# Neighbourhood attention trunk: two more output row tiles by seven products, shorter attention runs, loads and scalings in another order

## The chip, the cores and the metric

The kernel runs on one core of a Trainium2 chip. The metric is the device time of one execution in microseconds. The engines are named as in the profile: PE is TensorE (PEld its weight loads), DVE is VectorE, ACT is ScalarE, POOL is GpSimd, and SP issues nearly all DMA transfers.

## The reference

One layer of an encoder: RMSNorm, one projection to q, k, v and a gate, 2-D neighbourhood attention on a grid of 32 rows by 64 columns, gate, output projection, residual, final RMSNorm. 2048 tokens, 1024 features, 16 heads of 64, float32.

```python
h = rmsnorm(x, norm_0)
q, k, v, gate = split(h @ w_in_0, 4)             # (2048, 1024) each
# query (r, c) of a head sees 8 rows x 16 columns of keys, clipped at the edges:
#   rs = clip(r - 4, 0, 24), cs = clip(c - 8, 0, 48)
s = q . k / 8 + rpb[head, kr - r + 7, kc - c + 15]
o = softmax(s) @ v
x = x + (o * silu(gate)) @ w_out_0
out = rmsnorm(x, norm_f)
```

## The kernel before

**Products in two halves, and seven instead of eight.** Every float32 operand is split into a high and a low part, and a product is high x high, high x low, low x high: three matmuls for 128 rows of depth. Most products are done in 2 x 2 blocks by seven block products instead of eight (`seven_products`, and `rows_by_seven` for the output projection). What is not done so is called plain: a plain group of 128 x 512 results takes 8 x 3 = 24 matmuls.

**Stages.** `stage_one` and `stage_two` project the first and the second half of the tokens. Then come 32 attention runs and one more turn of the loop to empty the pipeline. Behind them `rows_by_seven` does the output projection of those row tiles (128 tokens each, 16 in all) that are not plain. Work that attention leaves room for is the plain part: 288 matmuls of the last projections (`projections`) and then the output projection of the first `PLAIN` = 4 row tiles (`outputs`), 48 matmuls each.

**An attention run** is a pair (p, T): p is a pair of heads (8), T a quarter of the tokens (4). `order` lists them: T = 1 and 0 for every p, then T = 2 and 3. A turn m of the loop emits, in this order:
- `begin(m)`: the loads for later: q, k and bias tables of run m+1, v of run m, the gate (sgt) of run m-1. `later_loads` gives each a lag, counted in matmuls of 512 columns, after which SP's list gets it. SP takes its list strictly in order.
- `feed`: plain matmuls, `amount[m]` of them, in pieces; a group's result is evacuated by ACT (and DVE for the gate).
- `normalise(2m-1)`: the softmax's scaling of the second quad of the run before. A quad is half a run, four of its eight column groups; it has two halves of rows with two tensors each, so four scalings.
- pieces of later operands (`consume`, `split_rows`): ACT makes the high part (woh, gh), DVE the low part (wol, gl).
- `turns(m-1)`: 48 transposes in three steps (ph), copied to SBUF by ACT and DVE, three copies each (pta).
- `scores(2m)` and `scores(2m+1)`: 64 matmuls; DVE adds the bias table (em) and finds the extreme in the same instruction, ACT takes the exponential and its sum; a callback scales the first quad (`normalise(2m)`) when its sums are there.
- `values(m-1)`: 36 matmuls that need all six copies; DVE multiplies by the gate (og), and SP stores og to `ogd`.

T = 1 and 2 use the middle table for both halves; T = 0 and 3 use a smaller one (184 instead of 253 elements a row) for one half. In `normalise` before, the first quad's four scalings run on POOL; of the second quad's, one is POOL's, one ACT's and two DVE's.

**The stage behind.** `land_first`, `land_rest`, `land_T2` and `land_T4` load the split blocks of w_out (T1 to T4); `load_rows_of` loads a row tile's half from `ogd`. Of the seven products the sixth (P=6) uses T2; it is the first that does, as the seventh product of the stage.

Of the kernel before, what the change touches and what calls it, by code (L numbers as in the profile page):

```python
# [11 lines left out]
F32 = mybir.dt.float32  # L12
# [20 lines left out]
PLAIN = 4  # L33
# [28 lines left out]
def build(ctx, tc, x, xr, xt, wg, bias, w_out, n0, nf, out):  # L62
# [7 lines left out]
    ogd = [dram.tile([128, 4, NP, 128], F32, name=f"ogd{T}") for T in range(4)]  # L70
# [1120 lines left out]
    def projections():  # L1191
        for n, (kind, j, ph, c) in enumerate(halves):
            state["half"] = n
            w = (KINDS[kind] + j, ph)
            for a in range(2):
                if n == len(halves) - 5 and a == 0:
                    for k in range(RES_EARLY):
                        load_res(*turns_[k])
                if n == len(halves) - 1:
                    if a == 0:  # L1200
                        store(("ogl",), 20, lambda: (load_og(0), load_og(1)))
# [12 lines left out]
    order = [(p, T) for p in range(NP) for T in (1, 0)] + [(p, T) for p in range(NP - 2) for T in (2, 3)]  # L1214
# [4 lines left out]
    def load_k(p, T):  # L1219
        r0, r1, more = PARTS[T]  # L1220
        base = 12 * (T > 1)
        a, b = r0 * GW, r1 * GW + more
        must(*[("k", p, c) for c in range(a // 512, (b + 511) // 512)])

        def keys():
            if T in (1, 2):
                khalf.clear()
                KT[p, T // 2] = (kp([128, 2048], F32, "kt") if p % 2 == 0 else mkp([128, 1536], F32, "kt"))[:, :1344]
            t = KT[p, T // 2]
            if T == 2:  # L1230
                nc.gpsimd.memset(t[:, 1280:1288], 0.0)
            nc.sync.dma_start(t[:, a - base * GW:b - base * GW], kd[p][:, a:b])

        return keys
# [25 lines left out]
    def load_bias(p, T):  # L1260
# [3 lines left out]
        EM[p, T // 2, kind] = []  # L1264
        for quad in range(2):
            t = mp([128, 512], F32, "em")[:, :w]
            EM[p, T // 2, kind].append([t[:, :w // 2], t[:, w // 2:]])
            o = TABLE_AT[kind] + quad * w
            fs.append(lambda t=t, o=o, w=w: nc.sync.dma_start(t, bias[p, :, o:o + w]))
# [28 lines left out]
    def scores(i, between=None):  # L1298
# [16 lines left out]
        for half, (u, n) in enumerate(HALF_ROWS[T]):  # L1315
            xs_ = [by_column(X[quad, half, s], HALF_ROWS[T][half]) for s in range(2)]
            table = EM[p, T // 2, kinds_of[T][half]][quad]
# [12 lines left out]
    def normalise(i, both=False, between=None):  # L1330
        st = ST.pop(i)
        nc.vector.reciprocal(st[:, 8:12], st[:, 4:8])  # L1332
        _, T, quad = pairs[i]
        for half in range(2):
            for s in range(2):
                o = 8 + 2 * half + s
                t = by_column(X[quad, half, s], HALF_ROWS[T][half])
                if both and half:
                    nc.vector.tensor_scalar(t, t, st[:, o:o + 1], None, op0=OP.mult)
                elif both and s:  # L1340
                    nc.scalar.activation(t, t, AF.Copy, scale=st[:, o:o + 1])
                else:
                    nc.gpsimd.tensor_scalar(t, t, st[:, o:o + 1], 1.0, op0=OP.mult, op1=OP.mult)  # L1343
        if between:
            between()
# [25 lines left out]
    def values(m):  # L1371
# [18 lines left out]
        def keep():  # L1390
            nc.sync.dma_start(ogd[T][:, :, p], og.rearrange("p (i q) -> p i q", i=4))
# [22 lines left out]
    def load_og(n):  # L1414
# [3 lines left out]
        nc.sync.dma_start(t, ogd[T][:, i])  # L1418
# [16 lines left out]

    def add_rows(n, j, ps):
# [4 lines left out]
        y, st = (raw if j and n < 1 else ev)([128, 512], F32, "y"), Y[n][1]  # L1441
# [20 lines left out]
        def square():  # L1462
            nc.scalar.activation(xr, y, AF.Square, scale=0.5 ** 0.5, accum_out=st[:, j:j + 1])
            squared[0] += 1
# [67 lines left out]
    turns_ = [(0, 0), (1, 0), (2, 0), (0, 1), (1, 1), (2, 1), (3, 0), (3, 1)]  # L1532
# [104 lines left out]
    def load_rows_of(m, f, home=None):  # L1637
# [4 lines left out]
        nc.sync.dma_start(A[m, f].rearrange("p (k q) -> p k q", k=4), ogd[T][:, i, 4 * half:4 * half + 4])  # L1642
# [109 lines left out]
    dense, end_of_it = 13.5, 24  # L1752
    amount = [dense] * 25
# [4 lines left out]
    HEAD = 5  # L1758
    amount += [(96 * (12 - len(units_two)) + 48 * PLAIN - sum(amount) - first - end_of_it) / (cycles - 25)] * (cycles - 25) + [end_of_it - 6]
# [51 lines left out]
    for m in range(cycles + 1):  # L1811
        a = amount[m] - 8
        begin(m)
        feed(HEAD)
        if m:
            due_here = []
            quiet[0] = True
            if a < 12 and m > 8 and m % 2:
                normalise(2 * m - 1, True, lambda: due_here.append(split_rows() or consume(1, turn=True)))
            else:  # L1820
                normalise(2 * m - 1, True)
# [30 lines left out]
        else:  # L1852
# [3 lines left out]
            scores(2 * m + 1, lambda: normalise(2 * m))  # L1856
# [44 lines left out]
```

## Time and profile before

| | |
|---|---|
| median of 3 runs | 994.46 us (993.22 to 995.1) |
| the profiled execution | 991.77 us, span 989.8 us |
| PE busy | 979.6 us, 99% of the span |
| DVE, ACT, POOL busy | 757.3, 532.5, 148.1 us |
| attention | about 562 to 870 us |
| the stage behind it | from 869.15 us, 504 matmuls |

The span is the time from the first to the last instruction; the rest of an execution lies around it. A row of a list in order of time gives the start in us from the span's start, the length, the engine and line, what is written and read, and in brackets how long the engine was idle before and what ended that. Several alike are merged with their count.

### The profile page before, as it was taken

The numbers are of one execution on the slowest core, as the hardware profiler recorded it, in microseconds if no ns is written. First come the engines' busy times: TensorE is split into PE (matmuls) and PEld (weight loads), VectorE is DVE, ScalarE is ACT, GpSimd is POOL, SyncE is SP. The second block draws the span as 40 slices with busy tenths as digits, with TensorE's granted clock in tenths as the row PEclk, the third lists the DMA queues.
The fourth block names the chain that finished last, engine by engine and source line by source line (L and its number), as shares of the span: only waits on it lengthen the run. The fifth ranks groups of instructions, "written<-read, shape, count | busy, mean of one in ns | idle before, by whom it ended". The sixth has DMA issues, their size and how long they took to land.

```text
span 989.8 us, 22264 instructions
## 1 busy us (share of the span) xinstructions
PE 979.6 (99%) x8172; PEld 797.4 (81%) x8172; DVE 757.3 (77%) x1703; ACT 532.5 (54%) x1310; POOL 148.1 (15%) x396
## 2 busy tenths in 40 slices
PE   9999999999999999999999999999999999999997
PEld 7888888888788888888888777778778777888886
DVE  5899888988565876766776577778878878877866
ACT  7773245465435342333433377677778776653443
POOL 0000001232100000000000033333333332311110
PEclk9999999999999999999999999999999999999999
DMA  8943547777957936657455899988999988997754
GB/s 287 334 131 104 197 130 251 250 224 253 350 179 216 293 117 183 206 165 241 166 184 188 229 275 278 270 260 265 296 287 294 286 227 265 304 369 188 204 148 117
DMA packets 149228, 227.89 MB, mean 230 GB/s; under 512 B 13312, under 2 KB 65792, under 8 KB 149120
## 3 DMA queue, kind: packets, MB, share of 16 engines
q1 hardware_dynamic: 146096, 221.37, 71.0%
q0 software_dynamic: 2592, 4.72, 2.8%
q8 instruction: 64, 1.05, 0.4%
q10 hardware_dynamic: 432, 0.40, 0.1%
q14 instruction: 44, 0.36, 0.1%
HBM read 160.37 MB, written 66.06 MB: 229 GB/s over the span
## 4 chain that ended last, share of the span: by engine, by line
PE 95%; DMA 3%; ACT 1%; DVE 1%; issue 0%; SPq 0%; ACTq 0%
PE pp L440 40%; PE pv L606 13%; PE py L1681 12%; PE o L1384 7%; PE s L1311 5%; PE ph L1361 4%; PE pv L721 2%; PE pp L384 2%; PE pp L388 2%; PE pp L386 2%; DMA kt<-kd 2%; PE po L1586 1%; PE po L1590 1%; PE po L1588 1%; DMA xr<-in_x_dram 1%; ACT x L1327 1%
## 5 line engine op out<-in xcount | busy, mean ns | idle before, releaser
L440 PE MATMUL pp<-h,f 128*128 128x512 f32 x576 | 185.3, 389 | 0.0
L440 PE MATMUL pp<-t,f 128*128 128x512 f32 x702 | 171.4, 389 | 0.0
L440 PEld LDWEIGHTS pp<-t,f 128*128 128x128 f32 x702 | 131.7, 188 | 27.6 <-DVE u L453 0.2
L1327 ACT ACTIVATE x<-x,st 128x253 f32<-128x253 f32 (+1 forms) x256 | 125.1, 496 | 32.9 <-DVE st L1320 32.9
L440 PEld LDWEIGHTS pp<-h,f 128*128 128x128 f32 x576 | 108.1, 188 | 22.6
L440 PE MATMUL pp<-l,f 128*128 128x512 f32 x288 | 112.1, 389 | 0.0
L1343 POOL TENSOR_SCALAR x<-x,st 128x253 f32<-128x253 f32 (+1 forms) x160 | 78.5, 510 | 130.5 <-DVE st L1332 127.1
L1320 DVE CUSTOM_DVE_ANT_0 x<-s,em 128x253 f32<-128x253 f32 (+1 forms) x256 | 87.3, 398 | 6.6 <-issue 4.5
L423 DVE TENSOR_TENSOR f<-raw,f 128x512 fp32r<-128x512 f32 x105 | 75.8, 727 | 20.0 <-ACT f L422 19.9
L1384 PEld LDWEIGHTS o<-pta,vt 120*64 120x64 f32 x1152 | 70.0, 137 | 18.4 <-issue 12.0
L1384 PE MATMUL o<-pta,vt 120*64 120x192 f32 (+2 forms) x1152 | 84.1, 299 | 0.0
L422 ACT ACTIVATE f<-raw 128x512 fp32r<-128x512 f32 x105 | 63.7, 623 | 36.2 <-DVE raw L429 22.0
L1365 DVE COPY pta<-ph 120x512 f32<-120x512 f32 x96 | 60.3, 684 | 13.6 <-PE ph L1361 13.1
L1367 ACT ACTIVATE pta<-ph 120x512 f32<-120x512 f32 x96 | 50.5, 599 | 33.8 <-PE ph L1361 33.6
L440 PEld LDWEIGHTS pp<-l,f 128*128 128x128 f32 x288 | 54.1, 188 | 11.2
L1681 PE MATMUL py<-woh,f 128*128 128x512 f32 x192 | 60.9, 390 | 0.0
L1311 PE MATMUL s<-kt,q 64*32 64x253 f32 (+1 forms) x2048 | 58.7, 362 | 2.2 <-DMA kt<-kd 1.7
L1361 PEld LDWEIGHTS ph<-ident,x 64*120 64x120 f32 x1536 | 47.6, 135 | 11.3 <-issue 10.6
L606 PE MATMUL pv<-wh,t 128*128 128x512 f32 x176 | 56.4, 390 | 0.1
L440 PE MATMUL pp<-sixths,f 128*128 128x512 f32 x198 | 52.7, 389 | 0.0
L461 POOL TENSOR_TENSOR tmp<-tmp,rb 128x512 f32<-128x512 f32 x18 | 28.4, 1580 | 158.0 <-DVE tmp L458 138.3
L1361 PE MATMUL ph<-ident,x 64*120 64x64 f32 x1536 | 52.0, 221 | 0.0
(230 smaller groups left out, 1883.7 us busy)
## 6 DMA issues: line engine op xcount, KB each, us to landing
raw<-in_wg_dram SPq DMA_DIRECT2D x124, 256.0 KB
vt<-vd SPq DMA_DIRECT2D x32, 480.0 KB
row<-in_xr_dram SPq DMA_DIRECT2D x32, 256.0 KB
vd<-v SPq DMA_DIRECT2D x32, 256.0 KB
sgd<-sg SPq DMA_DIRECT2D x32, 256.0 KB
q<-qd SPq DMA_DIRECT2D x32, 256.0 KB
sgt<-sgd SPq DMA_DIRECT2D x32, 256.0 KB
ogd<-og SPq DMA_DIRECT2D x32, 256.0 KB
```

Of the source, the lines that this page charges most:

```text
L422: nc.scalar.activation(t[:, 0], src, AF.Copy)
L423: nc.vector.tensor_tensor(t[:, 1], src, t[:, 0].bitcast(F32), OP.subtract)
L440: nc.tensor.matmul(B[n, P], t[:, int(m == 2), c], x[k][int(m == 1)], start=P in (1, 6, 5) and k == 0 and m == 0, stop=k == 3 and m == 2, s ...
L606: nc.tensor.matmul(p, a[:, o], b, start=P in (1, 6, 5) and k == 0 and m == 0, stop=k == 3 and m == 2, skip_group_check=True)
L1311: nc.tensor.matmul(places[half, s][h * 32:h * 32 + 32], qt[a, g * 64 + half * 32:g * 64 + half * 32 + 32], kt[a, o:o + n * GW].rearrange(" ...
L1320: nc.vector.tensor_tensor_reduce(xs_[s], places[half, s].rearrange("p (r c) -> p c r", c=WIDE), table[s].rearrange("p (c r) -> p c r", c=W ...
L1327: nc.scalar.activation(xs_[s], xs_[s], AF.Exp, bias=st[:, o:o + 1], scale=-1.0, accum_out=st[:, 4 + o:5 + o])
L1343: nc.gpsimd.tensor_scalar(t, t, st[:, o:o + 1], 1.0, op0=OP.mult, op1=OP.mult)
L1361: nc.tensor.transpose(ph[h][:k, o:o + 64], X[quad, half, s][q, at:at + k], ident[q, q])
L1365: nc.vector.tensor_copy(o, i_)
L1384: nc.tensor.matmul(o[s * 64:s * 64 + 64, g0 * 64:g1 * 64], vt[:k, strip, s * 64:s * 64 + 64], moving, start=strip == 0, stop=strip == 7, s ...
L1681: nc.tensor.matmul(B[m, P], t[:, a, c], b, start=P in (1, 6, 5) and k == 0 and i == 0, stop=k == 3 and i == 2, skip_group_check=True)
```

## The change

- `PLAIN` goes from 4 to 2: row tiles 2 and 3 become a seventh pair for `rows_by_seven`. Of the plain matmuls of `outputs` 96 of 192 are left.
- `amount`: 10 matmuls in the first 23 turns instead of 13.5 in 25, about 11.8 in those behind.
- `SHARED` = 3: for the first three p all four T stand together (1, 0, 2, 3), and the middle table loaded for T = 1 serves T = 2 as well. kt's two homes take turns by count.
- `begin`: all loads of a run first, in one list with lags of 0.5 steps: sgt, tables, q, k, v. They come ahead of the og store and of the plain work's loads.
- `normalise` by halves: a reciprocal and two scalings for each half. Of the second quad's second half DVE and ACT do one each, POOL does all other (six of eight).
- `ogd` is laid out [128, 8, 4, 128] instead of [128, 4, 8, 128]: the store of og is one piece of 2 KB a partition instead of four of 512 bytes, the loads of a row tile come in pieces of 512 bytes.
- `add_rows`: the y tiles all come from one pool; the square's count is taken 10 matmuls later, so the next residual is asked for later.

```diff
-PLAIN = 4
+PLAIN = 2
+SHARED = 3
...
-    ogd = [dram.tile([128, 4, NP, 128], F32, name=f"ogd{T}") for T in range(4)]
+    ogd = [dram.tile([128, NP, 4, 128], F32, name=f"ogd{T}") for T in range(4)]
...
-    order = [(p, T) for p in range(NP) for T in (1, 0)] + [(p, T) for p in range(NP - 2) for T in (2, 3)]
+    order = [(p, T) for p in range(SHARED) for T in (1, 0, 2, 3)]
+    order += [(p, T) for p in range(SHARED, NP) for T in (1, 0)] + [(p, T) for p in range(SHARED, NP - 2) for T in (2, 3)]
...
-                KT[p, T // 2] = (kp([128, 2048], F32, "kt") if p % 2 == 0 else mkp([128, 1536], F32, "kt"))[:, :1344]
+                KT[p, T // 2] = (mkp([128, 1536], F32, "kt") if len(KT) % 2 else kp([128, 2048], F32, "kt"))[:, :1344]
...
-    def load_bias(p, T):
+    def table_at(p, T, kind):
+        return p, 0 if p < SHARED else T // 2, kind
+
+    def load_bias(p, T, upto=2):
...
-        EM[p, T // 2, kind] = []
-        for quad in range(2):
+        got = EM.setdefault(table_at(p, T, kind), [])
+        for quad in range(len(got), upto):
...
-    def normalise(i, both=False, between=None):
-        st = ST.pop(i)
-        nc.vector.reciprocal(st[:, 8:12], st[:, 4:8])
+    def normalise(i, half):
+        st = ST[i]
         _, T, quad = pairs[i]
-        for half in range(2):
-            for s in range(2):
-                o = 8 + 2 * half + s
-                t = by_column(X[quad, half, s], HALF_ROWS[T][half])
-                if both and half:
-                    nc.vector.tensor_scalar(t, t, st[:, o:o + 1], None, op0=OP.mult)
-                elif both and s:
-                    nc.scalar.activation(t, t, AF.Copy, scale=st[:, o:o + 1])
-                else:
-                    nc.gpsimd.tensor_scalar(t, t, st[:, o:o + 1], 1.0, op0=OP.mult, op1=OP.mult)
...
+        o = 2 * half
+        nc.vector.reciprocal(st[:, 8 + o:10 + o], st[:, 4 + o:6 + o])
+        for s in range(2):
+            f = st[:, 8 + o + s:9 + o + s]
+            t = by_column(X[quad, half, s], HALF_ROWS[T][half])
+            if quad == 0 or half == 0:
+                nc.gpsimd.tensor_scalar(t, t, f, 1.0, op0=OP.mult, op1=OP.mult)
+            elif s:
+                nc.scalar.activation(t, t, AF.Copy, scale=f)
+            else:
+                nc.vector.tensor_scalar(t, t, f, None, op0=OP.mult)
...
-    dense, end_of_it = 13.5, 24
-    amount = [dense] * 25
+    dense, end_of_it = 10.0, 24
+    many = 23
+    amount = [dense] * many
...
-        if m >= 1:
-            later_loads([lambda: load_sg(*order[m - 1])], 1, 0)
+        fs = [lambda: load_sg(*order[m - 1])] if m else []
+        if m + 1 < cycles:
+            nx = order[m + 1]
+            fs += load_bias(*nx)
+            if order[m][0] < SHARED and order[m][1] == 2:
+                fs += load_bias(*order[m + 2], 1)
+            fs += [load_q(*nx), load_k(*nx)]
+        if m < cycles:
+            fs.append(lambda: load_v(*order[m]))
+        later_loads(fs, 0.5, 0.5)
...
-        if m < cycles:
-            later_loads([lambda: load_v(*order[m])], 4, 0)
-        if m + 1 < cycles:
-            nx = order[m + 1]
-            later_loads([load_q(*nx), load_k(*nx)], 7, 5)
-            later_loads(load_bias(*nx), 3, 1.5)
...
-        feed(HEAD)
+        feed(HALF_HEAD)
+        if m:
+            normalise(2 * m - 1, 0)
+        feed(HEAD - HALF_HEAD)
...
-            scores(2 * m + 1, lambda: normalise(2 * m))
+            scores(2 * m + 1, lambda: normalise(2 * m, 0))
+            normalise(2 * m, 1)
```

The program's order shows the change at three places. First SP's list in a run, before. Each transfer on SP waits on one of eight semaphores (DMAHW) in turn, that is, for the transfer eight places ahead of it; other waits stand behind.

```order
L1391 DMA ogd_85<-og 512x1x128 [waits DMAHW5_49,DVE_49]
L1250 DMA vt<-vd_84 120x1x1024 [waits DMAHW6_49,PE_49]
L1269 DMA em<-in_bias_dram 128x506 [waits DMAHW7_49]
L1241 DMA q<-qd_64 128x512 [waits DMAHW0_49]
L373 DMA qd_66<-q 128x512 [waits DMAHW1_49,Activation_49]
L1232 DMA kt<-kd_72 128x968 [waits DMAHW2_49]
```

And now:

```order
L1257 DMA sgt<-sgd_77 128x512 [waits DMAHW3_49]
L1274 DMA em<-in_bias_dram 128x368 [waits DMAHW4_49]
L1274 DMA em<-in_bias_dram 128x368 [waits DMAHW5_49]
L1274 DMA em<-in_bias_dram 128x506 [waits DMAHW6_49]
L1243 DMA q<-qd_61 128x512 [waits DMAHW7_49,PE_49]
L1234 DMA kt<-kd_69 128x256 [waits DMAHW0_49]
L1252 DMA vt<-vd_83 120x1x1024 [waits DMAHW1_49,PE_49]
L1394 DMA ogd_86<-og 128x512 [waits DMAHW2_49,DVE_49]
```

The og store, which waits for DVE, stood ahead of v, q and k; now it stands behind them, and q waits for TensorE. Second, DVE's list in a run in which two pieces of w_out are split, before:

```order
L1388 TENSOR_TENSOR og<-o,sgt 128x512 [waits DMAHW2_49,PE_49]
L1332 RECIPROCAL st<-st 128x4 [waits Activation_49]
L1339 TENSOR_SCALAR x_5203<-x_5203,st 128x23x11 [waits DVE_49]
L1339 TENSOR_SCALAR x_5205<-x_5205,st 128x23x11
L191 TENSOR_TENSOR wol<-raw,woh 128x512 [waits Activation_49] x2
L1365 COPY pta<-ph_7592 120x2x4x64 [waits PE_49]
```

And now, at the run that stands 17th (position 16, counted from 0):

```order
L1391 TENSOR_TENSOR og<-o,sgt 128x512 [waits DMAHW0_49,PE_49]
L1339 RECIPROCAL st<-st 128x2 [waits Activation_49] x2
L1348 TENSOR_SCALAR x_5203<-x_5203,st 128x23x11 [waits DVE_49]
L192 TENSOR_TENSOR wol<-raw,woh 128x512 [waits Activation_49] x2
L1368 COPY pta<-ph_8266 120x2x4x64 [waits PE_49]
```

One scaling is gone; the two pieces stand where they stood, between scaling and copies. Third, TensorE's list at the same run now, from the end of the values product to the first transpose:

```order
L1387 MATMUL o<-pta,vt 64x192 x10
L1387 MATMUL o<-pta,vt 64x128 x2
L389 MATMUL pp<-h,w 128x512
L385 MATMUL pp<-h,w 128x512
L387 MATMUL pp<-l,w 128x512
L389 MATMUL pp<-h,w 128x512
L385 MATMUL pp<-h,w 128x512
L387 MATMUL pp<-l,w 128x512
L389 MATMUL pp<-h,w 128x512
L1364 MATMUL ph_8265<-ident,x_5191 120x64 [waits PE_49,Pool_49]
```

Seven plain matmuls stand there; 13 or 14 stood there in most runs before. Counted over the whole list, the runs at positions 0 to 31 now have 39, 10, 10, 12, 8, 10 (ten times), 13, 7, 13, 7, 10, 10, 10, 14, 10, 14, 10, 14, 11, 13, 9, 15 and 15 of them ahead of their transposes.

More of the change, by code (lines that the diff above doesn't have):

```diff
@@ L1316, in scores @@
             xs_ = [by_column(X[quad, half, s], HALF_ROWS[T][half]) for s in range(2)]
-            table = EM[p, T // 2, kinds_of[T][half]][quad]
+            table = EM[table_at(p, T, kinds_of[T][half])][quad]
             for s in range(2):
@@ L1440, in add_rows @@
             Y[n] = [None, None], tiny.tile([128, 8], F32, name="st3")
-        y, st = (raw if j and n < 1 else ev)([128, 512], F32, "y"), Y[n][1]
+        y, st = ev([128, 512], F32, "y"), Y[n][1]
         Y[n][0][j] = y
@@ L1641, in load_rows_of @@
         A[m, f] = (home or raw)([128, 512], F32, "raw")
-        nc.sync.dma_start(A[m, f].rearrange("p (k q) -> p k q", k=4), ogd[T][:, i, 4 * half:4 * half + 4])
+        nc.sync.dma_start(A[m, f].rearrange("p (k q) -> p k q", k=4), ogd[T][:, 4 * half:4 * half + 4, i])
     def form_rows(m, P):
```

25 lines of the change are left out of this document (12 added, 13 removed).

## The prediction

> **What bounds the kernel now.** I read the page's busy line first, then the chain that ended last, then TensorE's weight loads (PEld) between 560 and 870 us in order of time, since this is where the change works.
>
> ```profile
> span 989.8 us, 22264 instructions
> ...
> PE 979.6 (99%) x8172; PEld 797.4 (81%) x8172; DVE 757.3 (77%) x1703; ACT 532.5 (54%) x1310; POOL 148.1 (15%) x396
> ...
> 869.15 114.49 PE py L1681 x504
> ```
>
> TensorE is the bound. The last row is the stage behind attention in one piece: 504 products in 114.49 us, so a product of 128x512 takes 114.49/504 = 0.2272 us when nothing is waited for.
>
> In attention each run opens with 48 transposes (L1361); their starts show whether TensorE waited. Columns: start, length, engine, line.
>
> ```profile
> 593.66 1.49 PEld L1361 LDWEIGHTS ph<-ident,x 64*120 64x120 f32 x48 [0.35 <-issue]
> 603.38 1.49 PEld L1361 LDWEIGHTS ph<-ident,x 64*120 64x120 f32 x48 [0.35 <-issue]
> 612.52 1.49 PEld L1361 LDWEIGHTS ph<-ident,x 64*120 64x120 f32 x48 [0.35 <-issue]
> 621.66 1.49 PEld L1361 LDWEIGHTS ph<-ident,x 64*120 64x120 f32 x48 [0.35 <-issue]
> ...
> 640.40 1.49 PEld L1361 LDWEIGHTS ph<-ident,x 64*120 64x120 f32 x48 [0.35 <-issue]
> 649.10 1.49 PEld L1361 LDWEIGHTS ph<-ident,x 64*120 64x120 f32 x48 [0.35 <-POOL x L1343]
> ...
> 676.52 1.49 PEld L1361 LDWEIGHTS ph<-ident,x 64*120 64x120 f32 x48 [0.35 <-issue]
> ...
> 731.38 1.49 PEld L1361 LDWEIGHTS ph<-ident,x 64*120 64x120 f32 x48 [0.35 <-issue]
> ...
> 742.00 1.12 PEld L1361 LDWEIGHTS ph<-ident,x 64*120 64x120 f32 x36 [0.36 <-issue]
> ...
> 806.24 1.49 PEld L1361 LDWEIGHTS ph<-ident,x 64*120 64x120 f32 x48 [0.35 <-issue]
> ...
> 817.06 1.49 PEld L1361 LDWEIGHTS ph<-ident,x 64*120 64x120 f32 x48 [0.35 <-issue]
> ```
>
> By the program's order 13 plain products stand between 603.38 and 612.52 (scores of a T=1 run) and 14 between 612.52 and 621.66 (T=0). So attention's own share of an interval is 9.14 - 13 x 0.2272 = 6.19 us for T=1 and 2, and 9.14 - 14 x 0.2272 = 5.96 for T=0 and 3. Test: 11 products before 649.10 should give 6.19 + 2.50 = 8.69, and 8.70 stands there. Three are too long: 14 products before 603.38 by 0.58, 13 before 742.00 by 1.48, 14 (a T=2 run) before 817.06 by 1.45. Worked out alike, the one before 603's is over by 0.31 and the one behind 817 by 0.17, no other by more than 0.01. That is 4.0 us, all that TensorE loses in attention.
>
> ```profile
> PE s L1311 <- DMA kt<-kd: 1.7, 2, 1.4
> ...
> 733.50 1.94 PE L1311 MATMUL s<-kt,q 64*32 64x253 f32 x64 [0.48 <-PE ph L1361]
> ...
> 739.26 1.14 ACT L1430 ACTIVATE gh<-ograw 128x512 fp32r<-128x512 f32 x2
> 739.90 1.29 DVE L1431 TENSOR_TENSOR gl<-ograw,gh 128x512 fp32r<-128x512 f32 x2 [1.10 <-ACT gh L1430]
> ```
>
> Keys (kt) that landed late explain the intervals before 603 and 817; the one before 742 holds the first splitting of gathered rows, and 0.48 us behind the transposes that nothing in the profile explains.
>
> **What a run must wait for.** The run from 640.40, with the scores of a T=1 run:
>
> ```profile
> 641.16 1.89 DVE L1365 COPY pta<-ph 120x512 f32<-120x512 f32 x3 [2.34 <-PE ph L1361]
> ...
> 643.83 2.38 PEld L1384 LDWEIGHTS o<-pta,vt 120*64 120x64 f32 x36 [0.41 <-issue]
> ...
> 646.12 2.66 POOL L1343 TENSOR_SCALAR x<-x,st 128x253 f32<-128x253 f32 x5 [3.44 <-DVE st L1332]
> 646.60 0.69 DVE L1388 TENSOR_TENSOR og<-o,sgt 128x512 f32<-128x512 f32 x1
> 647.22 0.53 ACT L1327 ACTIVATE x<-x,st 128x253 f32<-128x253 f32 x1
> 648.08 0.53 ACT L1341 ACTIVATE x<-x,st 128x253 f32<-128x253 f32 x1 [0.24 <-DVE st L1332]
> 648.08 0.85 DVE L1339 TENSOR_SCALAR x<-x,st 128x253 f32<-128x253 f32 x2
> ```
>
> DVE's three copies of the transposes end 643.05 - 640.40 = 2.65 us behind the run's start; the values product (L1384) starts at 3.43. So copies may be late by about 0.65 us in such a run; in a T=0 or 3 run, whose scores take 0.23 less, by about 0.4. The last exponential begins at 6.82, and ACT's and DVE's scalings at 7.68.
>
> **The change, part by part.** *Products.* Two row tiles leave the plain form (2 x 2 x 24 = 96 products) and become one pair of seven products (84): 12 x 0.2272 = -2.73 us, all on TensorE's path. Attention gives up 96 x 0.2272 = 21.8 us, the last stage gains 19.1.
>
> *Scalings by halves.* POOL takes six scalings instead of five (2.66/5 = 0.53 each), but in three pairs: the first when half of the first quad is summed, about 4.9 us in, to 6.0; the second to 7.0; the third behind og (646.60 + 0.69, so 6.9) and a reciprocal, to 8.1. DVE does one scaling, done at 8.1 instead of 8.53; ACT's ends at 8.2 as before. The transposes need the last quarter 0.39 to 0.45 in, so a T=1 or 2 interval can be as short as about 7.8 us, a T=0 or 3 one 7.35 (there scalings begin at 7.20: 692.87 below, in the run from 685.67). With 10 products TensorE needs 6.19 + 2.27 = 8.46 and 8.23: covered by 0.65 to 0.9. With 7 products (two runs, at order positions 16 and 18) 7.78: a wait of 0.1. So the shorter runs alone cost nearly nothing. What is gone is the cover for other work:
>
> ```profile
> 684.61 1.14 ACT L190 ACTIVATE woh<-raw 128x512 fp32r<-128x512 f32 x2
> 685.26 1.30 DVE L191 TENSOR_TENSOR wol<-raw,woh 128x512 fp32r<-128x512 f32 x2 [0.22 <-ACT woh L190]
> 685.67 1.49 PEld L1361 LDWEIGHTS ph<-ident,x 64*120 64x120 f32 x48 [0.35 <-issue]
> 686.47 1.88 DVE L1365 COPY pta<-ph 120x512 f32<-120x512 f32 x3
> ...
> 692.87 0.80 DVE L1339 TENSOR_SCALAR x<-x,st 128x253 f32<-128x253 f32 x2
> ```
>
> Here two pieces of w_out are split between scaling and copies. The split ends at 686.56, which is 10.04 behind that run's start (676.52), and the copies fall due 0.80 behind the next start, 9.15 + 0.80 = 9.95: just in time with 13 products. The change keeps these pairs in DVE's order and takes products away. Position 16 has 7: next start 7.8, copies due at 8.6, DVE free at 10.04: 1.4 late, so the values product waits 1.4 - 0.4 = 1.0. Position 17 has 13 and is late by 0.3; 18 has 7: its scalings come 0.3 late, its copies 1.4, and 1.0 is waited again. Sum 2.4. The first six runs split one piece each (half of it: DVE free at about 9.4, due at 9.25): lates of 0 to 0.6, waits 0.3. Positions 24 to 29 split two row tiles (1.14 on ACT, 1.29 on DVE each) and seven pieces of w_out, with 14, 10, 14, 11, 13, 9 products; the worst is the run of 10 with three of them (DVE free at 11.1, due at 9.5: late by 1.6, wait 1.0). I work out 0.3, 0.4, 1.0, 0.3, 0.1, 0.4: 2.5. New waits 5.2 us; bounds 1.5 (only the scalings wait) and 8 (every lateness reaches TensorE in full).
>
> *Loads first.* In a run's list on SP, q, kt and vt now stand ahead of the og store.
>
> ```profile
> 650.66 1.71 PE L1311 MATMUL s<-kt,q 64*32 64x184 f32 x64
> ...
> 655.69 0.56 SPq L1391 DMA_DIRECT2D ogd<-og  x1
> ...
> 658.17 0.43 SPq L1232 DMA_DIRECT2D kt<-kd  x1
> ...
> 668.94 1.71 PE L1311 MATMUL s<-kt,q 64*32 64x184 f32 x64
> ```
>
> Before, kt went out 2.5 us behind og, 10.8 before its scores (668.94); now it only waits for q's buffer, free when the scores from 650.66 are done (652.4), 5.8 us earlier. Queued behind q's wait are kt, vt and og, none needed for over 10 us. I take the kt intervals as gone: -(0.31 + 0.58 + 1.45 + 0.17) = -2.5 (bounds 0 and -2.5). Of the 1.48 before 742 the unexplained 0.48 stays; 1.0 goes, since the new waits above cost the split anew.
>
> *Tables, og layout, DMA.*
>
> ```profile
> 562.00:870.00 308.00, 305.43 (x5216) 242.35 (x5215) 245.96 (x855) 228.63 (x713) 99.43 (x345) 1.00 0.91 274
> ...
> 384.00:388.00 4.00, 4.00 (x19) 3.30 (x19) 2.35 (x5) 0.63 (x1) 0.00 (x0) 1.00 0.22 66
> ...
> 255.00:275.00 20.00, 19.73 (x86) 15.78 (x85) 12.38 (x19) 8.61 (x17) 3.32 (x2) 1.00 1.05 366
> ```
>
> The last two columns are the DMA's busy share and GB/s. From 384 one 256 KB store in 512-byte pieces takes 0.22 x 4 = 0.88 us; at 255 (pieces of 1 to 2 KB) 256 KB take 0.75. Attention holds 0.91 x 308 = 280 us of DMA. Gone are 6 tables (4.4), 32 x 0.13 by og's longer pieces, 8 outputs and residuals and two gathered tiles (9): 263 of 286 us, 0.92. The DMA does not become the bound, and these edits cost nothing.
>
> In the last stage ten loads ahead of the T2 pieces now come in 512-byte pieces: 1.3 us more, against four output stores fewer, 3.0.
>
> ```profile
> 881.55 0.32 SPq L1610 DMA_DIRECT2D wol<-wodT  x1
> ...
> 883.54 3.50 SPq L1610 DMA_DIRECT2D sixths<-wodT  x6
> ```
>
> The last T2 piece is out at 881.55 and landed when the sixth of the sixths, eight places on, was issued (by 887.0); it is needed at 869.15 + 81 x 0.2272 = 887.6. So no wait.
>
> The sum: -2.73 - 2.5 - 1.0 + 5.2 = -1.0. The profiled execution took 991.77, its span 989.8 and 1.97 around it, and would take 990.8; it lies 2.7 below the median shown, 994.46, which becomes 993.4.
>
> **POOL beside DVE.**
>
> ```profile
> L1343 POOL TENSOR_SCALAR x<-x,st x160: 426/494/1017, 569.4 to 861.7; 128x253 f32<-128x253 f32 x120, 128x184 f32<-128x184 f32 x40
> ```
>
> One scaling took twice the median (1017 against 494 ns), so POOL can be held by about 0.5. The Trainium skill, page "SBUF — State Buffer", section "SBUF: two separate sides", says that DVE and GpSimd share a port pair as an exclusive lock for a whole instruction, when the DVE operation is in a two-port mode or has two SBUF inputs. By that rule every third pair on POOL, which now runs beside DVE's scaling, would be held, and the time is that of the third rival below; the trace agrees only at its maximum, since five scalings beside two of DVE's took 2.66 us, 0.53 each.
>
> **Rivals.** (1) Lateness is absorbed, new waits 1.5: -2.73 - 3.5 + 1.5 = -4.7, 989.8. For it: the pairs of w_out at 685 cost nothing. Against: they had 13 products. (2) kt is late still, since SP's eight places in flight and not its order held it: +2.5, 995.9. Against: 0.92 of DMA leaves no more room than 0.91. (3) The other side: the third pair on POOL sets the transposes. It ends at 8.1 and is needed 0.33 into them, at 8.79 with 10 products; held for two DVE operations (1.0) it comes 0.3 late, and 0.2 a run over 24 runs give +4.8: 998.2. It decides from 0.7 of hold. Against: the median. (4) 512-byte reads cost double (1.5 instead of 0.75): T2 comes 7.5 - 3.0 - 0.6 late, +3.9: 997.3.
>
> **Numbers.** 0.2% of 994 is 2.0 us, about what a measurement of this kernel can tell from no change. Chances: forecast 0.52 (own range 991.5 to 995.3, a fifth of it under 992.5), rival 1 0.26, 2 0.05, 3 0.12, 4 0.05. Faster 0.26 + 0.10 = 0.36; slower 0.12 + 0.05 = 0.17; same 0.47. The range goes from 988.8, which is rival 1 with 1.0 of its 1.5 us of waits gone as well, to 997.4, just past rival 4; left out are rival 3 in its larger part (0.09) and the ends of the rest.
>
> **What would show it.** Starts of the transposes 8.46 and 8.23 apart with 10 products; no TensorE wait on kt; values products (L1387 then) started late by about 1 us behind the runs of 7 products; 588 products in 133.6 us behind attention. I am wrong if runs of 10 without splits are longer, or if the runs at positions 16 to 19 and 24 to 29 lose under 2 us together.

## The result

| | executions | median | ratio to the kernel before, 95% interval |
|---|---|---|---|
| before, first set | 7 | 993.22 us (991.24 to 995.1) | |
| changed | 7 | 1000.38 us (995.55 to 1007.18) | 1.0074 [1.0051, 1.0097] |
| before, second set | 23 | 992.33 us (989.98 to 996.56) | |
| changed, second set | 12 | 997.26 us (993.04 to 1005.24) | 1.0055 [1.0033, 1.0077] |

The changed kernel is slower by 5 to 7 us, where 993.4 (range 988.8 to 997.4) was forecast. Its executions also spread over 12 us in each set, those of the kernel before over 4 in the first and under 7 in the second. The two profiled executions stand at both ends of that spread: 1007.18 us in the first set, which is the profile that this section reads, and 993.04 in the second.

### The profile page after: what moved, and what is told of

Read it like the earlier page. It is cut to its first block, busy times and chain, and to the rows that moved or that the text cites. A ratio compares the mean times of both kernels' runs of the same rounds, so it can differ in the third digit from the quotient of the medians.

```text
span 1005.4 us, 22361 instructions
## 1 busy us (share of the span) xinstructions
PE 981.5 (98%) x8160; PEld 798.6 (79%) x8160; DVE 748.5 (74%) x1734; ACT 535.4 (53%) x1317; POOL 162.7 (16%) x431
## 4 chain that ended last, share of the span: by engine, by line
PE 83%; DMA 10%; DVE 2%; ACT 2%; issue 1%; SPq 1%; POOL 0%; ACTq 0%; DVEq 0%
PE pp L441 40%; PE pv L607 13%; PE py L1687 11%; PE o L1387 5%; PE s L1316 3%; DMA vt<-vd 3%; PE ph L1364 3%; DMA ogd<-og 3%; PE pv L722 2%; DMA kt<-kd 1%; PE pp L389 1%; PE pp L385 1%; PE pp L387 1%; ACT x L1332 1%; DVE x L1325 1%
## 5 line engine op out<-in xcount | busy, mean ns | idle before, releaser
L1344 POOL TENSOR_SCALAR x<-x,st 128x253 f32<-128x253 f32 (+1 forms) x192 | 89.6, 490 | 125.7 <-DVE st L1339 120.8
L1387 PE MATMUL o<-pta,vt 120*64 120x192 f32 (+2 forms) x1152 | 84.6, 299 | 9.4 <-DVE st L1325 4.0
L1387 PEld LDWEIGHTS o<-pta,vt 120*64 120x64 f32 x1152 | 72.9, 137 | 26.1 <-issue 12.6
L1687 PE MATMUL py<-woh,f 128*128 128x512 f32 x224 | 71.2, 390 | 0.0
L1316 PE MATMUL s<-kt,q 64*32 64x253 f32 (+1 forms) x2048 | 60.0, 364 | 1.5 <-issue 1.2
L1364 PEld LDWEIGHTS ph<-ident,x 64*120 64x120 f32 x1536 | 49.1, 137 | 12.8 <-issue 8.5
L1364 PE MATMUL ph<-ident,x 64*120 64x64 f32 x1536 | 54.0, 224 | 0.9 <-POOL x L1344 0.9
```

Source lines behind the costliest of these rows:

```text
L1316: nc.tensor.matmul(places[half, s][h * 32:h * 32 + 32], qt[a, g * 64 + half * 32:g * 64 + half * 32 + 32], kt[a, o:o + n * GW].rearrange(" ...
L1344: nc.gpsimd.tensor_scalar(t, t, f, 1.0, op0=OP.mult, op1=OP.mult)
L1364: nc.tensor.transpose(ph[h][:k, o:o + 64], X[quad, half, s][q, at:at + k], ident[q, q])
L1387: nc.tensor.matmul(o[s * 64:s * 64 + 64, g0 * 64:g1 * 64], vt[:k, strip, s * 64:s * 64 + 64], moving, start=strip == 0, stop=strip == 7, s ...
L1687: nc.tensor.matmul(B[m, P], t[:, a, c], b, start=P in (1, 6, 5) and k == 0 and i == 0, stop=k == 3 and i == 2, skip_group_check=True)
```

## The profile after

The page of the changed kernel, span and busy line:

```profile
span 1005.4 us, 22361 instructions
...
PE 981.5 (98%) x8160; PEld 798.6 (79%) x8160; DVE 748.5 (74%) x1734; ACT 535.4 (53%) x1317; POOL 162.7 (16%) x431
```

TensorE is as busy as before (981.5 against 979.6 us) in a span that is 15.6 us longer: it waits. TensorE's weight loads in order of time (start, length, engine, line; in brackets the idle time before and what ended it): transposes are L1364, the values product L1387.

```profile
660.27 1.49 PEld L1364 LDWEIGHTS ph<-ident,x 64*120 64x120 f32 x48 [0.35 <-issue]
...
668.51 1.49 PEld L1364 LDWEIGHTS ph<-ident,x 64*120 64x120 f32 x48 [0.35 <-issue]
...
676.98 1.49 PEld L1364 LDWEIGHTS ph<-ident,x 64*120 64x120 f32 x48 [0.35 <-issue]
...
730.04 1.49 PEld L1364 LDWEIGHTS ph<-ident,x 64*120 64x120 f32 x48 [0.35 <-POOL x L1344]
...
734.94 2.40 PEld L1387 LDWEIGHTS o<-pta,vt 120*64 120x64 f32 x36 [2.11 <-ACT x L1332]
...
740.01 1.49 PEld L1364 LDWEIGHTS ph<-ident,x 64*120 64x120 f32 x48 [0.35 <-issue]
742.83 1.49 PEld L1316 LDWEIGHTS s<-kt,q 64*32 64x32 f32 x64 [1.32 <-issue]
746.37 2.40 PEld L1387 LDWEIGHTS o<-pta,vt 120*64 120x64 f32 x36 [2.05 <-ACT x L1332]
...
751.44 1.49 PEld L1364 LDWEIGHTS ph<-ident,x 64*120 64x120 f32 x48 [0.35 <-POOL kt L1233]
```

The first three starts are 8.24 and 8.47 apart: a run of 10 products takes what was forecast (8.23 and 8.46). The last three are 9.97 and 11.43 apart, also with 10 products, and both times the values product stood still for 2 us, the second time behind scores (L1316) that had already waited 1.3 for keys. The name behind the idle time of 2 us, ACT's exponential, was long done by then; v landed at 734.84 and at 746.27, each time 0.1 us ahead of its product. The chain that ended last shows such waits as well. Start and length of its transfers, from issue to landing:

```profile
684.26 13.49 DMA vt<-vd
...
716.13 9.42 DMA vt<-vd
...
772.52 8.31 DMA ogd<-og
...
782.86 6.54 DMA sgt<-sgd
...
813.92 10.16 DMA vt<-vd
```

The v issued at 684.26 landed at 697.75, and the values product of that run started at 697.86: it waited for v. Matching each issue of v with its landing in this trace, v goes out 10.3 us ahead of its product in the median run (14.2 before) and is 9.4 us on the way (7.9 before); in 10 of 32 runs it lands less than 0.2 us ahead, in none before.

What SP itself waits for, the largest rows, first before, then after (us in total, times, longest):

```profile
SPq L1391 <- DVE og L1388: 46.7, 19, 5.4
SPq L1391 <- DMA vt<-vd: 24.0, 9, 3.5
```

```profile
SPq L1252 <- DMA vt<-vd: 28.0, 9, 3.8
SPq L1234 <- DMA vt<-vd: 24.2, 7, 4.2
SPq L1394 <- DMA vt<-vd: 20.5, 7, 4.2
SPq L1421 <- DMA ogd<-og: 7.8, 1, 7.8
```

Before, SP waited about as long for DVE, that is, for work to send (62 us from 562 to 860), as for an earlier transfer to land, so that one of its eight semaphores comes free (67). Now it waits for landings above all: these waits add up to 146 us (115 in the second set's profile), those for DVE to 8. The row of 7.8 us is one event: the load of gathered rows (L1421) must wait until the og store from 772.52 has landed (780.83), the gate behind it in the list goes out at 782.86, and it lands at 789.40 where DVE's og had waited for it for 5.1 us. TensorE stood still for 3.8 us, which made one interval 4.2 us longer. Right behind that wait the granted clock was 0.5 for 3.41 us (PEclk, the third column from the right); the next 48 transposes took 2.81 instead of 1.63 us, and the next interval lost 1.6:

```profile
791.98:795.39 3.41, 3.41 (x64) 2.86 (x70) 2.58 (x4) 2.46 (x5) 1.26 (x10) 0.50 1.00 276
```

The first set's profile shows one such drop, the second set's none.

By the prediction's working (n x 0.2272 + 6.19 or 5.96, with n products), the intervals between transposes lose, in us (numbers count the 31 intervals):

| profiled execution of | 1st | 2 to 13 | 14 to 20 | 21 to 31 | all |
|---|---|---|---|---|---|
| before | 0 | 0.9 | 1.5 | 1.6 | 4.0 |
| changed (1007.18) | 1.6 | 1.9 | 7.7 | 10.1 | 21.2 |
| changed, second set (993.04) | 1.6 | 1.4 | 2.7 | 2.6 | 8.4 |

17.2 us more in attention, 2.7 less for the products and 1.3 more in the last stage (134.95 us for its 588 products) make the 15.6 by which the span grew, to 0.2.

## The experiments

Several kernels leave out or change part of the computation, as their expectations say. Ratios are to the kernel before on the same chip.

### Where v stands in the list

First thought: v is late because it now goes out last.

> The changed kernel once more, for a second profile of it beside the other runs of this set. Theory V (v, which now goes out last of a run's loads, lands only when the values product wants it): about 7 us above the kernel before, 998 to 1003, with the values product starting as v lands in about half of the runs. Theory F (the DMA queue as a whole is too full for runs this short, whatever its order): the same time, but other loads late as well. Theory S (pieces of w_out and gathered rows hold DVE and ACT): the same time, with late copies and v landed early.

```diff
# v_second
         fs = [lambda: load_sg(*order[m - 1])] if m else []
+        if m < cycles:
+            fs.append(lambda: load_v(*order[m]))
         ...
-        if m < cycles:
-            fs.append(lambda: load_v(*order[m]))
         later_loads(fs, 0.5, 0.5)
# old_list: the six calls of later_loads in the kernel before, in place of this list
# before_new_list: this list in the kernel before
```

> The changed kernel with one edit: v stands second in a run's list of loads (behind the gate, ahead of tables, q and keys) and not last. Theory V: v lands 3 us or more ahead of its product, the losses in attention fall from 21 us of the profiled execution to 5 to 9, and the time comes to 991 to 995. Theory F: tables, q or keys are late instead, and the time stays above 997. Theory S: nothing moves by more than 2 us.

> The changed kernel with the loads of a run in the order and with the lags of the kernel before (gate, v, q, keys, tables); all else as changed. Theory V: v is early again, 991 to 996, with one or two runs that wait for keys as before. Theory F: above 997, since runs are as short and the bytes are the same. Theory S: within 2 us of the changed kernel.

> The kernel before with one edit: a run's loads in the changed kernel's order (gate, tables, q, keys, v last, all ahead of the store of og). Runs stay at 13.5 plain products. Theory V: v goes out about 10 us ahead of its product instead of 13.5 and lands with 1 to 3 us to spare in runs of 9.15 us, so little is lost: 0 to 3 us above the kernel before, and the waits for keys (2.5 us) go. Theory F: no loss, up to 2.5 us less. Theory S: no change beyond the waits for keys.

Measured: the changed kernel again 1.0055; v_second 1005.90 us, 1.0134 [1.0097, 1.0170]; old_list 1008.57, 1.0142 [1.0110, 1.0175]; before_new_list 993.97, 1.0010 [0.9994, 1.0027]. Theory V fell: with v early the kernel is slower still. v_second's waits of TensorE:

```profile
PE s L1316 <- DMA kt<-kd: 11.1, 9, 2.1
```

v now lands 5.4 us ahead of its product in the median, and the keys have lost what v gained: in 12 runs they land within 0.2 us of their scores (1 in the changed kernel, 5 before). The loads are late in whichever order they stand, and the changed order is the best of the three. In the kernel before, with runs of 13.5 products, the same list costs nothing that can be told, though v comes within 0.2 us of its product in three runs of its profiled execution.

### Short runs, and fewer bytes

> The kernel before with 11 instead of 13.5 plain products in each of its first 25 runs, and the rest (about 19 more a run) behind; lists, scalings, tables and PLAIN stay. Runs of 8.46 to 8.7 us instead of 9.15, the same bytes in each. Theories F and F8 (short runs outpace the DMA): the first 25 runs lose 5 us or more, on v, keys or gates, 996 to 1003. Theory S (only splits, scalings and lists cost): under 2 us, 992 to 995.

```diff
# before_short
-    dense, end_of_it = 13.5, 24
+    dense, end_of_it = 11.0, 24
```

Measured: 1001.92 us, 1.0076 [1.0055, 1.0097]. Nothing but shorter runs, ahead of longer ones, costs what the whole change costs. Its profiled execution loses 14.7 us, of them 3.8 and 4.2 in two intervals (4 and 22), where TensorE waited 2.1 and 2.8 us for keys:

```profile
PE s L1311 <- DMA kt<-kd: 5.3, 3, 2.8
```

The rest of these two is the clock, granted at 0.5 for 3.41 us right behind each wait (from 605.31 and 765.74).

> The changed kernel with one set of bias tables for all heads: 6 of 58 table loads are left, the other 52 (0.6 us of DMA each, 31 of about 262 us in attention) are left out, so the biases of most heads are not those of the reference. Theory D (the loads of a run take nearly as long as a run of 8.4 us, and what is late is a matter of order and luck): v, keys and gates land 4 us or more ahead, what is left in attention is 5 us at the splits and 1.6 at the first run, and the time comes to 992 to 995. Rival P (what costs is not the DMA but the shorter cover on TensorE, DVE and ACT): within 2 us of the changed kernel, 996 to 1001.

> The kernel before with one set of bias tables (58 of 64 table loads left out, biases wrong for most heads). Theory D: it had room, so only its waits for keys go, 2.5 of the 4.0 us that it loses in attention: 989 to 991. Rival P: no change.

```diff
# after_less (before_less likewise)
+    ONCE = {}
     def load_bias(p, T, upto=2):
...
-        got = EM.setdefault(table_at(p, T, kind), [])
+        if kind in ONCE:
+            EM[table_at(p, T, kind)] = ONCE[kind]
+            return []
+        got = ONCE[kind] = EM.setdefault(table_at(p, T, kind), [])
```

Measured: after_less 992.19 us, 1.0002 [0.9985, 1.0019]; before_less 991.88, 0.9989 [0.9971, 1.0006]. Theory D holds. 52 tables less take 5 to 7 us from the changed kernel; 58 less take about 1 from the kernel before, with an interval that reaches no change. A table left out takes away bytes and a place in SP's rotation of eight at once; which of the two counts, these two runs don't separate. DMA share (second to last column) in attention, first the changed kernel, then after_less:

```profile
562.00:858.00 296.00, 280.39 (x5024) 222.52 (x5024) 216.63 (x840) 218.50 (x690) 110.50 (x377) 0.99 0.88 259
```

```profile
562.00:846.00 284.00, 282.29 (x5073) 220.92 (x5057) 218.92 (x842) 219.03 (x693) 108.27 (x377) 1.00 0.78 235
```

At 0.88 SP stood before landings half of the time; at 0.78 it hardly does (21 us). What SP waits for in after_less:

```profile
SPq L1243 <- PE s L1321: 78.8, 28, 5.5
SPq L1252 <- PE o L1392: 41.8, 27, 6.5
```

These are waits for buffers that TensorE has yet to free, as they should be: the loads are ahead of the work. v lands 7.3 us and keys 9.7 us ahead in the median, no load is late, and 588 products behind attention take what they should:

```profile
848.61 133.53 PE py L1692 x588
```

### Why a share of 0.88 is full

In the trace of before, v's pieces (4096 bytes) seem to use half of the DMA: of the time in which pieces of that size are in flight, more than nine are in flight in 9% before and 2% in the changed kernel, and eight are the most frequent number. While one v was landing in the changed kernel (742.5 to 746.1) the share was 0.80. The Trainium skill, page "DMA: Bandwidth & Descriptors", section "Why a DMA increments its semaphore by 16 and not by 1", says that a transfer uses the largest number of engines up to 16 that divides the slowest dimension of both sides; v's is 8 x 15 rows in DRAM and 120 partitions here, so eight, and one row of 120 would give 15.

> The changed kernel with v's 120 rows of 4 KB read in the order in which they lie in DRAM, so that its access pattern is one row of 120 and not 8 x 15; bytes and pieces are the same, v's rows come to the product in another order, which is the part of the computation that it changes. In the traces at most 8 or 9 of v's pieces move at a time, and the DMA share falls to 0.78 while v is landing. Theory F8 (v runs on half of the DMA engines, and these are what is full in runs of 8.4 us): up to 15 or 16 of v's pieces move at a time, loads land 2 us or more earlier, the waits for v, keys and gates go, and the time comes to 989 to 993, the losses of the splits alone. Theory F (all DMA engines are full alike): no change, 995 to 1003.

> The kernel before with the same edit (v's rows come in another order; that part of the computation is changed). Its v landed 3.5 to 7 us ahead of its product, and it lost 4.0 us in attention, 2.5 of them on keys. Theory F8: those 2.5 us go at most, 989 to 993. Theory F: no change.

```diff
# after_v15, before_v15
-        rows = vd[...].rearrange("(r c s) d -> c r s d", c=8, s=8)[:, r0:r1]
+        rows = vd[...].rearrange("(r c s) d -> (r c) s d", c=8, s=8)[8 * r0:8 * r1]
```

Measured: before_v15 991.00 us, 0.9978 [0.9967, 0.9989]; after_v15 998.53, 1.0061 [1.0039, 1.0084]. The mechanism shows: more than nine pieces are in flight in 45% of that time and more than 15 in 4%, which agrees with the page's eight and 15. A transfer takes 6.0 us from issue to landing instead of 8.8 in the median (600 to 840 us; 8.1 in the second set's profile), SP's waits for landings fall from 146 to 49 us at a share of 0.89, v lands 8.1 us ahead and keys 8.4. The kernel before gains 2.2 us, as expected, though its profiled execution (992.23) still loses 3.7 in attention. The changed kernel does not, though no load is late: besides the losses that after_less has too, its profiled execution lost 4.1 and 1.8 us in two intervals (7 and 3) with a halt in the middle of a values product. TensorE's rows at the larger:

```profile
630.21 0.71 PE L1387 MATMUL o<-pta,vt 120*64 120x128 f32 x9
633.07 3.84 PE L1387 MATMUL o<-pta,vt 120*64 120x64 f32 x27 [2.15 <-issue]
```

After nine of 36 matmuls it waits for nothing that the profile names, with v and all copies there. The other 27 run slowly, with the granted clock at 0.5 from 633.40 on, for 3.41 us again: of the 4.1 us about 2 are the halt's and the rest the clock's.

> after_less with v's rows read in the order of DRAM, as in after_v15 (v's order and most biases wrong). after_v15 had every load early and still stood at 998.5, with two halts of 4.1 and 1.8 us in the middle of a values product, at the 7th and 3rd transposes, where the profile names no load and a piece of instructions lands near the halt's end. If these halts come of TensorE's instructions waiting behind a full DMA: they go, 5 to 6 us lost in attention, 990 to 993 like after_less. If they belong to v read in that way whatever the load: they stay, 995 to 999.

Its edits are those of after_less and after_v15 together. Measured: 993.05 us, 0.9999 [0.9989, 1.0008], with 8.1 us lost, of them 1.8 at the 3rd and 0.7 at the 2nd interval. The expectation for a full DMA named the time (990 to 993) but not this: a halt at the same place stays at a share of 0.80. So the halts need no share of 0.9; after_less_no_low, below, has one too (2.1 us).

The traces show what TensorE waits for there: its own instructions. They come through a DMA queue of their own:

```profile
q8 instruction: 64, 1.05, 0.4%
```

That is 64 packets of 16 KB, and the trace has 16,534 records of TensorE (weight loads, matmuls, semaphores), about 256 to a packet. Counting these records in order, I find 22 halts of over 0.3 us inside a values product in the 17 profiled executions. All 22 fall on the 193rd or 194th record of a block of 256, and all end 1.3 to 1.6 us behind the landing of such a packet: the one above goes on at 633.07, and a packet landed at 631.55. Nowhere in the traces does TensorE pass such a place less than 1.2 us behind its packet. The profiled execution of before has no halt of this kind, that of the changed kernel two (1.1 and 0.4 us), after_v15 four (5.1 together). Seven of the 22 come at the 3rd or 7th interval of the changed kernel and its variants, the others elsewhere: 2.7 us at the 15th in old_list, 1.0 at the 2nd in before_v15. The Trainium skill, page "Runtime: NRT & Kernel Launch", section "Instruction fetch mechanics", says that an engine's instructions are fetched in blocks of 16 KiB and that crossing a block is mostly hidden; the blocks agree with these traces, and here some crossings are not hidden. Why a packet comes late in one execution and not in another, no run shows.

### v through the other queue

> The changed kernel with v loaded through GpSimd's queue instead of SP's, bytes and result unchanged. Theory F8: if that queue deals the eight parts of a transfer to other engines than SP's does, the low half is relieved and v no longer stands in SP's rotation of eight: 990 to 996, less what the descriptors cost on POOL (a GpSimd instruction a run, put at 1 us, which may hold the scalings). Theory F: no gain, 996 or more.

> The kernel before with v loaded through GpSimd's queue, result unchanged. In the changed kernel this edit let keys, gates and queries land 2 to 5 us earlier and left v 4 us of margin. Theory D: the waits for keys go, 1 to 3 us less than before, 990 to 992. Rival P: no change, or about 1 us more where POOL's scalings wait for the descriptors.

```diff
# after_v_pool, before_v_pool
-        nc.sync.dma_start(t[:8 * TALL], rows)
+        nc.gpsimd.dma_start(t[:8 * TALL], rows)
```

Measured: after_v_pool 997.11 us, 1.0035 [1.0017, 1.0053]; before_v_pool 1002.24, 1.0104 [1.0086, 1.0121]. The first is a little better than the changed kernel (intervals that overlap), with v 4.2 and keys 7.6 us ahead. The second missed its expectation by 10 us: keys land within 0.2 us of their scores in five runs there, and its profiled execution has six halts for instructions, five inside values products and one among the plain matmuls; the four longest add up to 5.5 us. Why that queue helps the one and hurts the other was not pursued.

### Scalings and splits

> after_less with the scalings as in the kernel before (one reciprocal and four scalings a quad, five a run on POOL). If scalings by halves cost nothing, as the prediction had it: within 1 us of after_less. If POOL's third pair holds the transposes (the prediction's rival): 1 to 5 us less. If the halves are what lets runs of 10 products go without a wait: 5 us more or above, the transposes waiting for POOL in most runs.

```diff
# after_less_old_scale: normalise and its calls as in the kernel before
-        feed(HALF_HEAD)
-        if m:
-            normalise(2 * m - 1, 0)
-        feed(HEAD - HALF_HEAD)
+        feed(HEAD)
...
-            normalise(2 * m - 1, 1)
+            normalise(2 * m - 1, True)
...
-            scores(2 * m + 1, lambda: normalise(2 * m, 0))
-            normalise(2 * m, 1)
+            scores(2 * m + 1, lambda: normalise(2 * m))
```

Measured: 992.82 us, 0.9993 [0.9980, 1.0006], against 992.19: scalings by halves cost and bring nothing that can be told, and the first interval loses 1.6 us with the old ones as well.

> after_less with one more edit: the low parts of w_out and of the gathered rows are set to zero on DVE instead of being worked out (same tiles, same places in the order, no wait for ACT's high part and a shorter instruction), so these products lose their low part. In after_less 3.9 us were still lost between the 14th and the 30th transposes, always at the same places and of the same size, and 1.6 at the first run. Theory S (there the splits make DVE's copies late, as the prediction's term of 5.2 us had it): most of the 3.9 us goes, lost in attention 2 to 3.5 us, time 2 to 3 us under after_less (988 to 991). Rival: the runs of 7 products are too short by themselves, or POOL's third pair: the losses stay, and the time too.

```diff
# after_less_no_low (w_out; the gathered rows likewise)
-            nc.vector.tensor_tensor(l, t, h.bitcast(F32), OP.subtract)
+            nc.vector.memset(l.bitcast(F32), 0.0)
```

Measured: 990.56 us, 0.9978 [0.9966, 0.9990]. In intervals 21 to 31 after_less lost 2.3 us, this kernel 0.2. Over all intervals its profiled execution still lost 5.8, and not the 2 to 3.5 expected, since 2.3 came at the 7th, with a halt for instructions. The worst run there, transposes, values product and next transposes, first in after_less, then here:

```profile
787.11 1.49 PEld L1369 LDWEIGHTS ph<-ident,x 64*120 64x120 f32 x48 [0.35 <-POOL x L1349]
...
791.22 2.38 PEld L1392 LDWEIGHTS o<-pta,vt 120*64 120x64 f32 x36 [0.41 <-issue]
...
797.16 1.49 PEld L1369 LDWEIGHTS ph<-ident,x 64*120 64x120 f32 x48 [0.35 <-issue]
```

```profile
789.62 1.49 PEld L1369 LDWEIGHTS ph<-ident,x 64*120 64x120 f32 x48 [0.35 <-issue]
...
793.07 2.38 PEld L1392 LDWEIGHTS o<-pta,vt 120*64 120x64 f32 x36 [0.41 <-issue]
...
799.02 1.49 PEld L1369 LDWEIGHTS ph<-ident,x 64*120 64x120 f32 x48 [0.35 <-issue]
```

The product starts 4.11 us behind the transposes where copies are late, 3.45 where they aren't, and the interval falls from 10.05 to 9.40. So the late copies come of the splits there. In intervals 14 to 20 hardly anything changed (1.7 and 1.6): at the runs of 7 products ACT's two high parts, 1.14 us, still stand ahead of its copies, and DVE's two zeros take 1.02 us where the splits took 1.29.

### The rest of the change alone

> The changed kernel with its first two edits undone: four plain row tiles and 13.5 plain products a run as before, and tables loaded as before; left of the change are the loads of a run first, the scalings by halves and the layout of ogd. Theory D (only runs made shorter outpace the DMA): within 2.5 us of the kernel before, 990 to 995, v with 1 to 4 us to spare. Rival L (the new list, the scalings or the layout cost by themselves): 996 or more.

```diff
# after_plain4
-PLAIN = 2
+PLAIN = 4
-SHARED = 3
+SHARED = 0
-    dense, end_of_it = 10.0, 24
-    many = 23
+    dense, end_of_it = 13.5, 24
+    many = 25
```

(with the order of the plain tiles' halves and the lag of the first gathered rows as before). Measured: 992.94 us, 1.0013 [0.9999, 1.0026], 1.8 us lost in attention, v 5.6 and keys 7.0 us ahead, at a DMA share of 0.88 as in the changed kernel. List, scalings and layout take the waits for keys away and cost nothing that can be told; the time is spent where runs are made shorter. No kernel with the reference's result was faster than the kernel before. v spread over more engines, in the right order, was not tried.

## Why the prediction was wrong, point by point

- **The DMA: the step that failed.** The prediction took the mean share, 0.91 before and 0.92 worked out for after, as room to spare ("The DMA does not become the bound, and these edits cost nothing"). after_less puts 5 to 7 us on it, most of the miss. The share came out at 0.88 while SP waited for landings half of the time: a mean share said nothing of whether a load lands in time. The same 0.88 costs nothing in after_plain4, whose runs are longer, and before_short shows that the kernel before had little to spare. That v keeps eight engines is shown to lengthen the way of all loads; that this alone makes the miss is not, since after_v15 has no late load and stays at 1.0061. Rival 2 had the right symptom (loads late since places in flight hold them), but only for keys, 2.5 us and a chance of 0.05, and its counter-argument was the same mean.
- **"None needed for over 10 us".** It counted from issue and left out the way: 8.5 us from issue to landing in the changed kernel, 7.4 before (medians, 562 to 858 us). A load issued 10.3 us ahead lands 1 us ahead. v, the first to be needed and now the last in the list, was not looked at.
- **Products: right.** 588 of them in 133.53 us (after_less; forecast 133.6), undisturbed runs of 10 in 8.47 and 8.23.
- **Waits for keys gone (-2.5): right by itself** (no keys within 0.2 us of their scores in the profiled execution of the second set or in after_plain4, one in the first set's), but in the short runs TensorE waits for v instead. The 0.48 us that the prediction left unexplained (before 742) were keys too: they landed at 733.41, the scores started at 733.50.
- **Splits (5.2): nearly right in size.** after_less loses 4.2 us in intervals 2 to 31. From 21 on it is 2.3 against 2.5 forecast, and shown to be the splits; at 14 to 20 it is 1.7 against 2.4, with that cause only argued. "Lose under 2 us together" did not come about.
- **Missed: the first interval, 1.6 us.** In the midst of its transposes TensorE waits 0.9 us for POOL's scaling (574.5). The loss is there with old and new scalings, 0.9 with 11 products a run (before_short) and 0 with 13.5. That fewer products ahead of the first transposes cause it fits, and was not tried by itself.
- **Missed: the last stage,** 1.3 us longer than forecast in the first profile, 0.5 in the second, as forecast in after_less. In the first, T2's last piece landed as it was wanted (at 883.42; the weight load waited 0.46 us for it). The prediction had 0.6 us of margin there. The longer stop, 0.6 us at 887.52, is a wait for DVE's u (L1699), which ran 1.7 us later in the stage than in after_less; why was not followed.
- **Missed: two costs that the sum has no term for.** TensorE's halts for instructions (inside values products 1.5 us in the first profile and 0.9 in the second) and the clock behind a long wait (1.6 us in the first).
- **POOL's third pair (rival 3): no.** after_less_old_scale has the old pairs and the same time, and the median scaling on POOL takes 490 ns (494 before). Nor 512-byte reads (rival 4): the last stage of after_less has them and takes what was forecast.

With loads out of the way the sum holds: -2.7 for the products, -4.0 for the old losses, +5.8 for the new ones make -0.9; the span of after_less is 988.5 against 989.8, so -1.3.

## What to carry to other kernels

A transfer's share of the DMA is not its room: read in the trace what the issuing queue waits for (work, buffers, or landings) and how long a load is on its way, and count every load's margin from its landing to its first use before you shorten the work that hides it. When loads are late in one order, another order moves the wait; here only fewer bytes, more engines to a transfer or longer runs took it away, and with more engines the time did not follow. When an engine halts with all its operands there, count its instructions: a halt that always falls on the same place of a block is a wait for the instructions themselves.

## What the runs showed of the hardware

- A 480 KB load in 120 rows of 4 KB kept at most about eight pieces in flight read as 8 x 15 rows, and up to about 15 read as 120, and the median way of all transfers fell from 8.8 to 6.0 us, at DMA shares of 0.88 and 0.89.
- With SP waiting for landings half of the time, loads and stores of 256 KB were 8.1 to 9.0 us on the way in the median (q, gate, og in the changed kernel), though by the prediction's row such a transfer is 0.75 us of DMA.
- The same program ran from 993 to 1007 us. In the profiled executions at these two ends v landed 2.9 and 0.8 us ahead of its product in the median run.
- TensorE halted for up to 2.7 us inside a product whose operands were all there. All 22 such halts of over 0.3 us in values products fall on the same place of a block of 256 of its instructions, 1.3 to 1.6 us behind the landing of 16 KB of instructions, at DMA shares of 0.80 as well as 0.89.
- In attention the granted clock fell to 0.5 seven times in the 17 profiled executions, for 3.41 us (once 6.83), each time in or right behind a wait of TensorE of 2.08 us or more. Three waits of 2.0 to 2.3 us had no such drop.
